# Turning a block ahead of the next scores, dealing the convolution's taps more thinly, and turning tokens by products with diagonals

## The chip, the cores and the metric

The kernel runs on one core of one Trainium2 chip. TensorE (PE) multiplies matrices; VectorE (DVE), ScalarE (ACT) and GpSimd (POOL) work on elements; SyncE (SP) issues the transfers. PE reads its operands from SBUF and writes its products to PSUM banks, which DVE or ACT must empty before they are written again. The metric is the device time of one execution in microseconds, lower being better. Beside the runs stands one profiled execution, from which all durations below come.

## The reference

One step of a streaming encoder: 1024 new frames of a prompt (`x_prompt`) and 32 frames of running streams (`x_sample`), all with 1024 channels. Two branches share one normalised input and one wide projection.

```python
h = rmsnorm(x, norm_g)                            # x / root of the mean square, times g
q = rmsnorm(h @ w_q, q_g) * 64 ** -0.5            # 16 heads of 64
k = rmsnorm(h @ w_k, k_g);  v = h @ w_v
logf = log_sigmoid(h @ w_f + b_f)                 # forget gates; c = cumsum(logf)
u = (h @ w_ua) * sigmoid(h @ w_ub)
ga, gb, ma, mb = (h @ w for w in gate weights)
o = softmax(q k^T + c_q - c_k, causal) v          # by blocks of 128 queries
conv = depthwise causal convolution of u, 31 taps, + b_dw
ya = (o * silu(ga)) @ w_pa
yb = (silu(layernorm(conv, ln_g, ln_b)) * silu(gb)) @ w_pb
y = x + (sigmoid(ma) * ya + sigmoid(mb) * yb) @ w_out
```

The running streams attend to 512 cached keys each besides their own frames. Everything is asked for in f32.

## The kernel before, in words

The projections are computed with f16 halves. A token matrix is split into a high part `xh` and a rest `xl`, a weight tile into `wh` and `wl`, and each product is the sum of three matmuls: xh by wh, xh by wl, xl by wh (all of them stand in `mms`, L183). The tokens are 1024 + 32 = 1056 columns, worked in three chunks of 352; so a "beat" is three matmuls of 352 columns.

**The opening** (`x_split`, up to some 46 us). The tokens arrive as nine tiles `xtok` of 128 tokens by 1024 channels (the ninth has 32 tokens). They must be normalised and turned, so that channels lie on the partitions. For each tile the sum of squares is taken, and its reciprocal root lands in a column of `rs9` (`root`, then `newton`: L509 to L511). `scale` then multiplies half a tile, 128 x 512, by its roots in place (L541): twelve such halves on DVE and six on POOL. `x_split` takes the tiles in three groups of 256, 384 and 416 columns, each in eight slices of 128 channels (`kt`): PE turns the slice of each tile in the group (`nc.tensor.transpose`, L576, against the identity `ident`) into one bank `ptx`; ACT makes xh of it, DVE makes xl (L579); and the first two weight tiles' products with what is ready (L183) follow a few slices behind (`drain`). The `jobs` of a call are lists, by slice, of what is written between; among them are the scalings and the splitting of the weights (L141).

**Projections and attention.** Up to about 570 us PE runs projections. From there to about 1055 us it runs attention: `seq` lists 132 steps, 16 heads by 8 blocks of 128 queries and four steps of the running streams (`Sample`). Step n of the loop at the end of the attention does, in this order: the scores of step n + 3 (`start`, L1121 and L1122, into a bank pair `psS`, of which there are two; DVE then adds the mask, L1124, and takes the negated maximum `nm`, L1126); loads for heads to come; `turn` of step n, which turns the block of probabilities `P` in pieces of 128 x 128 on PE (L1153) into banks `ptr2`, of which there are two (pool `psT`, shared with the values' `po` and the layer norm's `psn`), and copies them to `pt` (L1156), the first four pieces on ACT, the others on DVE; the exponential of step n + 3 (`soft`, ACT, L1133); the normalising of step n + 2 (`norm`: a reciprocal on DVE, L1138, and the product of P with it on POOL, L1139); two beats of a gate's projection as filler; after every second block the values (L1172); two more beats; and one piece of the layer norm, once the convolution is done.

**The convolution's taps** are work for DVE alone: each is one multiply-add over 1086 columns (L371), and they are dealt out by `beat`. Each beat adds `pace["rate"]` to a credit, and each tap takes one off. In attention the rate is `R_A`. The last tap releases the layer norm, whose sums over channels are products `psn` (L1202).

**What sets the order.** PE, DVE and ACT follow the order in which the code is written; in attention SP does too. POOL's order is made by the framework. So an instruction that waits holds up all that is written behind it on its engine.

Of the kernel before, what the change touches and what calls it, by code (L numbers as in the profile page):

```python
# [30 lines left out]
LNO = ((0,), (1, 2), (3,), (4, 5), (6,), (7,), ())  # L31
LNEXP = "natural_log_exp_and_others"
NFILL = 22
R_U, R_V, R_QK, R_G, R_A = 0.21, 0.18, 0.165, 0.23, 0.2
NWARM = 34
HT = TT // 2
HC = HT // 2
# [16 lines left out]
def build(tc, xT, xt, wv, wf, ckT, cv, clT, stT, vec, cst, yT, kT, vO, lfO, cpT, csT):  # L54
# [35 lines left out]
    class Batch:  # L90
# [46 lines left out]
        def high(self, i, wh, raw, ks):  # L137
            nc.scalar.mul(wh[:, ks, :], raw[:, ks, :], self.s[:, i:i + 1])  # L138
# [393 lines left out]
        nc.scalar.activation(y, y, AF.Exp, scale=-0.5)  # L532
        return lambda: newton(rs, v, y)

    def scale(t, h, pool=False):
        r = rows(t)
        x, f = xtok[t][:r, half[h]], rs9[:r, t:t + 1]
        if pool:
            nc.gpsimd.tensor_scalar(x, x, f, 1.0, op0=ALU.mult, op1=ALU.mult)
        else:  # L540
            nc.vector.tensor_scalar(x, x, f, None, op0=ALU.mult)  # L541

    behind = [], []

# [5 lines left out]
    def x_split(c, ws, u, jobs):  # L550


        o, n = XCH[c]
        sl = slice(o, o + n)
        pss = [pj.tile([128, 512], F32, name="pj", tag="pj") for _ in range(2)]

        def project(i, kt):
            mms(pss[i][:, :n], ws[i], X, XL, sl, range(kt, kt + 1), kt == 0, kt == KT - 1)
            if kt < KT - 1:
                return  # L560
            if i == 0:
                for a, b in pieces(o, n):
                    nc.scalar.mul(u[:, b], pss[0][:, a], recs[0].inv)
                return
            nc.vector.tensor_scalar(ua0[:, sl], pss[1][:, :n], recs[1].inv, None, op0=ALU.mult)
            if c == 2:
                for o2, n2, a2 in PCS:
                    b = slice(30 + o2, 30 + o2 + n2)
                    nc.scalar.activation(u[:, b], u[:, b], AF.Sigmoid)
                    nc.vector.tensor_mul(u[:, b], ua0[:, a2:a2 + n2], u[:, b])  # L570

        for kt in range(KT):
            pt = tr.tile([128, 512], F32, name="ptx", tag="tr") if kt % 3 == 2 else st.tile([128, 512], F32, name="ptx", tag="st")
            for j in range((n + 127) // 128):
                r = min(128, n - 128 * j)
                nc.tensor.transpose(pt[:, 128 * j:128 * j + r],  # L576
                                    xtok[o // 128 + j][:r, 128 * kt:128 * kt + 128], ident[:r, :r])
            nc.scalar.mul(xh[:, kt, sl], pt[:, :n], gs[:, kt:kt + 1])
            nc.vector.scalar_tensor_tensor(xl[:, kt, sl], pt[:, :n], gs[:, kt:kt + 1], xh[:, kt, sl],  # L579
                                           op0=ALU.mult, op1=ALU.subtract)  # L580
            for job in jobs.get(kt, ()):
                job()
            for i in range(2):
                behind[i].append(lambda i=i, kt=kt: project(i, kt))
            drain((2, 5 if c == 0 else 2))
# [29 lines left out]
    top(0)  # L615
    total(1)
    step()
    scale(0, 0)
    scale(1, 0, True)
    scale(1, 1, True)  # L620
    scale(0, 1)
    known(0)
    steps_of = {}

# [14 lines left out]
    for f in range(8):  # L639
# [17 lines left out]
        2: [lambda: high(0, 1), lambda: low(0, 1)],  # L657
        3: [lambda: total(2), lambda: known(1), lambda: squares(4)],
        4: [lambda: high(1, 0), lambda: low(1, 0), lambda: rooted(2, 3), lambda: high(0, 2)],
        5: [lambda: steps_of[2](), lambda: scale(2, 0), lambda: scale(3, 0, True), lambda: scale(4, 0), lambda: low(0, 2)],  # L660
        6: [lambda: scale(3, 1, True), lambda: scale(2, 1), lambda: high(1, 1), lambda: low(1, 1)],
        7: [lambda: scale(4, 1), lambda: high(1, 2), lambda: low(1, 2)]})
    x_split(1, ws0, u0, {
        0: [b1.load, b1.load, lambda: squares(5), lambda: squares(6, False)],
        1: [lambda: squares(7)],
        2: [lambda: squares(8)],
        3: [lambda: rooted(5, 4)],
        4: [lambda: steps_of[5](), lambda: scale(5, 0), lambda: scale(6, 0, True)],
        5: [lambda: scale(7, 0), lambda: scale(8, 0), lambda: scale(6, 1, True)],
        6: [lambda: scale(5, 1), lambda: scale(7, 1)],  # L670
        7: [lambda: scale(8, 1), lambda: b1.stage(0)]})
    x_split(2, ws0, u0, {0: [lambda: b1.stage(1)], 2: [consts], 3: [b1.total, b1.power],
                         4: [lambda: b1.split(0)], 5: [lambda: b1.rest(0, 0), lambda: b1.rest(0, 1)],
                         6: [lambda: b1.rest(0, 2), lambda: b1.split(1)]})
# [563 lines left out]
    for n in range(3):  # L1238
# [3 lines left out]
            seq[n - 1].norm()  # L1242
        fill((8, 4, 0)[n])
    for n, b in enumerate(seq):
        if n + 3 < len(seq):
            start(seq[n + 3])
        if n + 9 < len(seq) and getattr(seq[n + 9], "i", 1) == 0:
            seq[n + 9].head.load()
        if n + 6 < len(seq) and isinstance(seq[n + 6], Sample):
            seq[n + 6].load()  # L1250
        if getattr(b, "i", 0) == 3 and b.head.h + 1 < H:
            heads[b.head.h + 1].load_v()
        b.turn()
        if n + 3 < len(seq):
            seq[n + 3].soft()
        if n + 2 < len(seq):
            seq[n + 2].norm()
        some = 2 if isinstance(b, Sample) or b.i > 2 or b.head.h != 8 else 0
        fill(some)
        if n >= 2 and pending(seq[n - 2]):  # L1260
            seq[n - 2].values()
        fill(some)
        if n >= 3 and isinstance(seq[n - 3], Sample):
            seq[n - 3].finish()
        if "ready" in sides:
            next(ln, None)
# [402 lines left out]
```

## Time and profile before

| | |
|---|---|
| median of 3 runs | 1346.9 us (1346.65 to 1347.09) |
| the profiled execution's own time | 1345.89 us |
| its span in the trace | 1344.1 us |
| mean clock of PE in it | 0.996 of full speed |
| PE busy | 1312.6 us, 98% of the span |
| DVE busy | 990.4 us, 74% |
| ACT busy | 719.0 us, 53% |
| POOL busy | 505.8 us, 38% |

The page divides the span among engines and gives, for each group of like instructions, the busy time, the mean time of one in ns, and behind the second bar the idle time of its engine just ahead of them, with what ended it. In the rows of a timeline the first number is the start in us from the span's beginning, the second the duration; what is in square brackets is the wait ahead of it and what ended it. In a row of windows the stretch's bounds come first, then its length, then for each engine the busy time with the count of its instructions.

### The profile page before, as it was taken

Reading aid. Unit: us, or ns where it says so; the run is one execution under the profiler, and the core shown is the slowest. Engines: PE = TensorE matmul, PEld = TensorE weight load, DVE = VectorE, ACT = ScalarE, POOL = GpSimd, SP = SyncE. Lnnn points to the kernel's source line nnn. Section 1 sums busy time; section 2 is a strip of 40 time slices with the busy share of each in tenths; the row PEclk is TensorE's granted clock in tenths of the full one; section 3 lists DMA queues with packets and bytes.
Section 4 is the critical chain, followed back from the end, with each engine's and each line's share of the span. In section 5 each row is a group of like instructions: output and inputs, shape, how many; then the busy total and the mean of one; then the engine's idle time right before and its main releaser. Section 6 shows DMA issues by size and latency. Waiting matters only on the chain.

```text
span 1344.1 us, 24837 instructions
## 1 busy us (share of the span) xinstructions
PE 1312.6 (98%) x9383; PEld 1003.1 (75%) x9383; DVE 990.4 (74%) x1532; ACT 719.0 (53%) x1362; POOL 505.8 (38%) x548
## 2 busy tenths in 40 slices
PE   8999999999999999999889998999999999999999
PEld 5687876666666666667567766777776699999998
DVE  6797879888999997987778866655554489166664
ACT  6644555757676743455555555655555566233320
POOL 2001124547484820243433442222222158255562
PEclk8999999999999999999999999999999999999999
DMA  6343233425352463535644643565452698544462
GB/s 251 98 140 104 93 112 118 139 82 187 95 180 87 162 166 109 160 90 155 165 109 123 186 132 99 147 179 132 131 152 54 240 313 262 176 128 146 142 190 69
DMA packets 113496, 194.97 MB, mean 145 GB/s; under 512 B 34080, under 2 KB 80032, under 8 KB 113376
## 3 DMA queue, kind: packets, MB, share of 16 engines
q1 hardware_dynamic: 113232, 193.31, 46.9%
q8 instruction: 74, 1.21, 0.4%
q14 instruction: 46, 0.38, 0.1%
q10 hardware_dynamic: 144, 0.07, 0.0%
HBM read 127.68 MB, written 65.64 MB: 144 GB/s over the span
## 4 chain that ended last, share of the span: by engine, by line
PE 82%; DVE 9%; ACT 3%; issue 2%; DMA 2%; SPq 1%; POOL 0%; DVEq 0%; ACTq 0%; POOLq 0%
PE pj L183 56%; PE pjv L761 6%; PE pj L1501 6%; PE po L1172 4%; PE ptr L1153 3%; DVE nm L1126 2%; DVE wl L141 2%; DVE y L371 2%; PE psS L1122 2%; PE psS L1121 2%; DMA ga<-s_ga 2%; ACT wh L138 1%; DVE psS L1124 1%; DMA s_q<-qh 1%; PE warm L477 1%
## 5 line engine op out<-in xcount | busy, mean ns | idle before, releaser
L183 PE MATMUL pj<-xh,wh 128*128 128x352 f16 (+2 forms) x1536 | 481.6, 314 | 2.3 <-ACT wh L138 1.4
L183 PE MATMUL pj<-xh,wl 128*128 128x352 f16 (+2 forms) x1536 | 481.2, 313 | 0.7 <-DVE wl L141 0.6
L183 PE MATMUL pj<-xl,wh 128*128 128x352 f16 (+2 forms) x1536 | 480.9, 313 | 0.5 <-DVE xl L579 0.4
L183 PEld LDWEIGHTS <-wh 128*128 128x128 f16 x3072 | 301.5, 98 | 162.1 <-issue 7.1
L371 DVE SCALAR_TENSOR_TENSOR y<-u,vec_t,y 128x1086 f32<-128x1086 f32 x240 | 346.8, 1446 | 12.0 <-ACT y L368 8.9
L1139 POOL TENSOR_SCALAR P<-P,nm 128x128 f32<-128x128 f32 (+7 forms) x128 | 129.9, 1015 | 279.9 <-DVE nm L1138 229.8
L183 PEld LDWEIGHTS <-wl 128*128 128x128 f16 x1536 | 150.5, 98 | 72.0 <-DVE wl L141 1.6
L141 DVE SCALAR_TENSOR_TENSOR wl<-raw,sc,wh 128x384 f16<-128x384 f32 (+1 forms) x192 | 128.2, 693 | 48.3 <-ACT wh L138 48.3
L1133 ACT ACTIVATE P<-psS,nm 128x128 f32<-128x128 f32 (+7 forms) x128 | 95.1, 743 | 113.3 <-DVE nm L1138 70.9
L1126 DVE TENSOR_REDUCE nm<-psS 128x1 f32<-128x128 f32 (+7 forms) x128 | 97.0, 758 | 12.5
L1153 PE MATMUL ptr<-ident,P 128*128 128x128 f32 x576 | 88.6, 276 | 17.3 <-DVE pt L1156 9.2
L175 POOL TENSOR_TENSOR wl<-raw,wh 128x384 fp32r<-128x384 f32 (+1 forms) x51 | 63.3, 1270 | 74.3 <-ACT wh L172 58.6
L1153 PEld LDWEIGHTS ptr<-ident,P 128*128 128x128 f32 x576 | 69.2, 141 | 28.2 <-DVE pt L1156 12.1
L1156 ACT COPY pt<-ptr 128x512 f32<-128x512 f32 (+3 forms) x128 | 64.3, 502 | 44.4 <-PE ptr L1153 43.2
L1121 PE MATMUL psS<-KB,QB 128*128 128x256 f32 (+2 forms) x192 | 81.8, 427 | 0.6 <-ACT P L1133 0.6
L880 POOL TENSOR_TENSOR sql<-sqf,sqh 128x352 fp32r<-128x352 f32 x48 | 57.0, 1187 | 65.8 <-ACT sqh L877 65.8
L138 ACT ACTIVATE wh<-raw,sc 128x1024 f16<-128x1024 f32 (+1 forms) x68 | 73.9, 1091 | 8.2 <-DVE sc L158 7.9
L1172 PE MATMUL po<-pt,V 128*64 128x256 f32 x640 | 72.8, 382 | 2.5 <-ACT pts L1078 1.7
L1124 DVE TENSOR_TENSOR psS<-psS,cmask 128x128 f32<-128x128 f32 x128 | 37.6, 294 | 46.0 <-PE psS L1122 45.6
L906 POOL TENSOR_TENSOR ql<-qn,qh 128x352 fp32r<-128x352 f32 (+1 forms) x48 | 67.8, 1429 | 6.6 <-ACT qh L905 6.5
L761 PE MATMUL pjv<-vwh,xh 128*128 128x260 f16 x256 | 70.1, 274 | 0.0
L761 PE MATMUL pjv<-vwl,xh 128*128 128x260 f16 x256 | 70.0, 273 | 0.0
(271 smaller groups left out, 2532.9 us busy)
## 6 DMA issues: line engine op xcount, KB each, us to landing
raw<-wf SPq DMA_DIRECT2D x92, 512.0 KB
QB<-s_q SPq DMA_DIRECT2D x32, 256.0 KB
KB<-s_k SPq DMA_DIRECT2D x32, 256.0 KB
kT<-qn SPq DMA_DIRECT2D x8, 528.0 KB
s_ga<-t SPq DMA_DIRECT2D x24, 176.0 KB
s_gb<-t SPq DMA_DIRECT2D x24, 176.0 KB
s_ma<-t SPq DMA_DIRECT2D x24, 176.0 KB
s_mb<-t SPq DMA_DIRECT2D x24, 176.0 KB
```

Of the source, the lines that this page charges most:

```text
L138: nc.scalar.mul(wh[:, ks, :], raw[:, ks, :], self.s[:, i:i + 1])
L141: nc.vector.scalar_tensor_tensor(wl[:, ks, :], raw[:, ks, :], self.s[:, i:i + 1], wh[:, ks, :], op0=ALU.mult, op1=ALU.subtract)
L183: nc.tensor.matmul(ps, a[:, kt, :], b(kt, sl), start=(first and n == 0), stop=(last and n == N - 1))
L371: t = nc.vector.scalar_tensor_tensor(y, u[:, i:i + CW], w, y, op0=ALU.mult, op1=ALU.add)
L761: nc.tensor.matmul(ps[:, :VC], a, b, start=(n == 0), stop=(n == 23))
L1121: nc.tensor.matmul(ps[:, b, :wm], QB[:, qsl], KB[:, ksl], start=True, stop=False)
L1126: nc.vector.tensor_reduce(nm[:, 0:1], ps[:, :nb, :w], axis=AX.XY, op=ALU.max, negate=True)
L1133: nc.scalar.activation(P[:, :nk].rearrange("p (b w) -> p b w", b=nb), ps[:, :nb, :w], AF.Exp, bias=nm[:, 0:1], accum_out=nm[:, 1:2])
L1139: nc.gpsimd.tensor_scalar(P[:, :nk], P[:, :nk], nm[:, 2:3], 1.0, op0=ALU.mult, op1=ALU.mult)
L1153: nc.tensor.transpose(pt[:, 128 * j:128 * j + 128], P[:, 128 * (4 * u + j):128 * (4 * u + j) + 128], ident)
L1172: nc.tensor.matmul(po[rows], V[:, j, :], parts[c][:, j, :], start=(c % 2 == 0 and j < 2), stop=(c % 2 == 1 and j >= 2 * c))
L1501: nc.tensor.matmul(pss[c][:, :HC], a[:, k, :], x, start=(not more and kt == 0 and n == 0), stop=(kt == 3 and n == 2), skip_group_check=more)
```

## The change

Three edits stand in the diff.

First, in each attention step `b.turn()` is written at the head of the step, ahead of the scores of step n + 3 and of the loads.

Second, `R_A` is 0.165 in place of 0.2.

Third, in the opening nothing scales the token tiles any more. `diag` makes, for each tile, a 128 x 128 f32 matrix with the tile's roots on its diagonal (DVE, the identity times a column of `rs9`), nine in all, and the turning of a slice is written as a matmul of the tile with its diagonal in place of a transpose against the identity: the product is the turned tile with each token's column times its root. There are 64 such products of 128 x 128 and eight of 32 tokens.

```diff
-R_U, R_V, R_QK, R_G, R_A = 0.21, 0.18, 0.165, 0.23, 0.2
+R_U, R_V, R_QK, R_G, R_A = 0.21, 0.18, 0.165, 0.23, 0.165
...
-    def scale(t, h, pool=False):
-        r = rows(t)
-        x, f = xtok[t][:r, half[h]], rs9[:r, t:t + 1]
-        if pool:
-            nc.gpsimd.tensor_scalar(x, x, f, 1.0, op0=ALU.mult, op1=ALU.mult)
-        else:
-            nc.vector.tensor_scalar(x, x, f, None, op0=ALU.mult)
+    diags = {}
+
+    def diag(*ts):
+        for t in ts:
+            r = rows(t)
+            diags[t] = xip.tile([128, 128], F32, name="diag", tag="diag", bufs=9)
+            nc.vector.tensor_scalar(diags[t][:r, :r], ident[:r, :r], rs9[:r, t:t + 1], None, op0=ALU.mult)
...
-                nc.tensor.transpose(pt[:, 128 * j:128 * j + r],
-                                    xtok[o // 128 + j][:r, 128 * kt:128 * kt + 128], ident[:r, :r])
+                t = o // 128 + j
+                nc.tensor.matmul(pt[:, 128 * j:128 * j + r], xtok[t][:r, 128 * kt:128 * kt + 128], diags[t][:r, :r],
+                                 start=True, stop=True)
...
-    scale(0, 0)
-    scale(1, 0, True)
-    scale(1, 1, True)
-    scale(0, 1)
+    diag(0, 1)
...
-        5: [lambda: steps_of[2](), lambda: scale(2, 0), lambda: scale(3, 0, True), lambda: scale(4, 0), lambda: low(0, 2)],
-        6: [lambda: scale(3, 1, True), lambda: scale(2, 1), lambda: high(1, 1), lambda: low(1, 1)],
-        7: [lambda: scale(4, 1), lambda: high(1, 2), lambda: low(1, 2)]})
+        5: [lambda: steps_of[2](), lambda: diag(2, 3, 4), lambda: low(0, 2)],
+        6: [lambda: high(1, 1), lambda: low(1, 1)],
+        7: [lambda: high(1, 2), lambda: low(1, 2)]})
...
-        4: [lambda: steps_of[5](), lambda: scale(5, 0), lambda: scale(6, 0, True)],
-        5: [lambda: scale(7, 0), lambda: scale(8, 0), lambda: scale(6, 1, True)],
-        6: [lambda: scale(5, 1), lambda: scale(7, 1)],
-        7: [lambda: scale(8, 1), lambda: b1.stage(0)]})
+        4: [lambda: steps_of[5](), lambda: diag(5, 6, 7, 8)],
+        7: [lambda: b1.stage(0)]})
...
     for n, b in enumerate(seq):
+        b.turn()
         if n + 3 < len(seq):
             start(seq[n + 3])
...
             heads[b.head.h + 1].load_v()
-        b.turn()
         if n + 3 < len(seq):
             seq[n + 3].soft()
```

How the instructions stand is shown at three places. The first is PE at the step of block 4 of head 0, between two beats of filler (L183): L1121 and L1122 are the scores of the block three steps ahead (two bank halves, two products each), L1153 the turning of block 4's five pieces (in the changed kernel the lines are L1117, L1118 and L1149). Before:

```order
L183 LDWEIGHTS wh
L183 MATMUL pj<-xl,wh 128x352
L1121 MATMUL psS<-KB,QB 128x512
L1122 MATMUL psS<-KA,QA 128x512
L1121 MATMUL psS<-KB,QB 128x512
L1122 MATMUL psS<-KA,QA 128x512
L1153 MATMUL ptr_7038<-ident,P 128x128 x4
L1153 MATMUL ptr_7044<-ident,P 128x128
L183 LDWEIGHTS wh
```

And changed:

```order
L183 LDWEIGHTS wh
L183 MATMUL pj<-xl,wh 128x352
L1149 MATMUL ptr_7029<-ident,P 128x128 x4
L1149 MATMUL ptr_7035<-ident,P 128x128
L1117 MATMUL psS<-KB,QB 128x512
L1118 MATMUL psS<-KA,QA 128x512
L1117 MATMUL psS<-KB,QB 128x512
L1118 MATMUL psS<-KA,QA 128x512
```

The turning's five pieces moved from behind the four products of the scores to ahead of them.

The second place is DVE in the steps of blocks 5 and 6 of head 0: L1124 adds the mask to the scores three steps ahead, L1126 takes their maximum, L1156 copies the turned pieces beyond the fourth, L1138 is the reciprocal for POOL's normalising, L141 splits a weight tile and L371 is a tap. Before:

```order
L141 SCALAR_TENSOR_TENSOR wl<-raw,sc,wh 128x384
L1124 TENSOR_TENSOR psS<-psS,cmask 128x128
L1126 TENSOR_REDUCE nm<-psS 128x1
L1156 COPY pt<-ptr_7084 128x2x128
L1138 RECIPROCAL nm<-nm 128x1
L141 SCALAR_TENSOR_TENSOR wl<-raw,sc,wh 128x256
L371 SCALAR_TENSOR_TENSOR y<-u,vec_t,y 128x1086
L1124 TENSOR_TENSOR psS<-psS,cmask 128x128
L1126 TENSOR_REDUCE nm<-psS 128x1
L1156 COPY pt<-ptr_7121 128x3x128
```

And changed:

```order
L141 SCALAR_TENSOR_TENSOR wl<-raw,sc,wh 128x384
L1152 COPY pt<-ptr_7077 128x2x128
L1120 TENSOR_TENSOR psS<-psS,cmask 128x128
L1122 TENSOR_REDUCE nm<-psS 128x1
L1134 RECIPROCAL nm<-nm 128x1
L141 SCALAR_TENSOR_TENSOR wl<-raw,sc,wh 128x256
L1152 COPY pt<-ptr_7113 128x3x128
L1120 TENSOR_TENSOR psS<-psS,cmask 128x128
L1122 TENSOR_REDUCE nm<-psS 128x1
```

The copy now stands ahead of the mask and the maximum, and the tap between the two steps has gone to a later place.

The third place is DVE in the opening, from the roots of tiles 2 to 4 (L511) through the next slices; one piece of the difference between the kernels:

```order
 L511 SCALAR_TENSOR_TENSOR rs_185<-rs_185,n_303 128x3
-L541 TENSOR_SCALAR xtok<-xtok,rs_185 128x512 x2
+L541 TENSOR_SCALAR diag<-ident,rs_185 128x128 x3
 L141 SCALAR_TENSOR_TENSOR wl_217<-raw_116,sc,wh_216 128x256
-L579 SCALAR_TENSOR_TENSOR xl<-ptx,gs,xh 128x256
-L541 TENSOR_SCALAR xtok<-xtok,rs_185 128x512
+L580 SCALAR_TENSOR_TENSOR xl<-ptx,gs,xh 128x256
 L141 SCALAR_TENSOR_TENSOR wl_219<-raw_117,sc,wh_218 128x384
-L579 SCALAR_TENSOR_TENSOR xl<-ptx,gs,xh 128x256
-L541 TENSOR_SCALAR xtok<-xtok,rs_185 128x512
+L580 SCALAR_TENSOR_TENSOR xl<-ptx,gs,xh 128x256
```

Four scalings of 512 columns became three diagonals of 128, and the xl of the next slices stand that much sooner; on PE the products keep the places of the transposes. Elsewhere the last tap stands in head 8 in place of head 6, and the layer norm's products `psn` in head 10 among beats of filler in place of head 8, where the code leaves the filler out in three steps (`b.head.h != 8`).

## The prediction

> **What bounds the kernel now.** First the profile page: the share of each engine, the chain that ended last, and the costliest group.
>
> ```profile
> span 1344.1 us, 24837 instructions
> PE 1312.6 (98%) x9383; PEld 1003.1 (75%) x9383; DVE 990.4 (74%) x1532; ACT 719.0 (53%) x1362; POOL 505.8 (38%) x548
> PE 82%; DVE 9%; ACT 3%; issue 2%; DMA 2%; SPq 1%; POOL 0%; DVEq 0%; ACTq 0%; POOLq 0%
> L183 PE MATMUL pj<-xh,wh 128*128 128x352 f16 (+2 forms) x1536 | 481.6, 314 | 2.3 <-ACT wh L138 1.4
> ```
>
> PE is busy in 1312.6 of 1344.1 us and carries 82% of the chain. So two things alone move the time: work that PE gets or loses, and its 31.5 us of idleness. Busy time by stretches tells where these lie (opening, then attention; the columns after the stretch are its length, then PE, PEld, DVE, ACT, POOL, the granted clock and the DMA).
>
> ```profile
> 10.00:20.00 10.00, 7.51 (x38) 4.89 (x37) 7.16 (x19) 8.55 (x21) 1.27 (x4) 0.66 1.04 390
> 20.00:30.00 10.00, 8.67 (x66) 6.41 (x65) 7.81 (x16) 6.73 (x16) 1.14 (x2) 1.00 0.36 147
> 30.00:40.00 10.00, 9.46 (x61) 5.94 (x59) 7.85 (x21) 6.92 (x13) 2.40 (x3) 1.00 0.00 1
> 40.00:50.00 10.00, 10.00 (x62) 6.03 (x61) 6.95 (x14) 6.20 (x10) 0.27 (x1) 1.00 0.19 57
> 570.00:700.00 130.00, 119.18 (x875) 85.67 (x875) 100.99 (x193) 71.15 (x155) 51.25 (x58) 1.00 0.47 127
> 700.00:800.00 100.00, 97.29 (x744) 70.44 (x741) 75.76 (x145) 56.70 (x121) 41.17 (x50) 1.00 0.55 153
> 800.00:900.00 100.00, 94.53 (x659) 68.61 (x658) 64.10 (x161) 59.45 (x135) 25.64 (x45) 0.98 0.51 136
> 900.00:1000.00 100.00, 99.42 (x754) 72.69 (x752) 53.11 (x131) 55.82 (x122) 24.63 (x48) 1.00 0.51 136
> 1000.00:1055.00 55.00, 53.43 (x426) 37.69 (x425) 27.97 (x65) 29.71 (x61) 12.44 (x19) 1.00 0.25 76
> ```
>
> In the opening PE fills up: idle 1.33 us in the second of these stretches, 0.54 in the third, nothing in the fourth. In attention it idles for 10.82 + 2.71 + 5.47 + 0.58 + 1.57 = 21.2 us. The waits of PE say on what: the whole run's group of turning products, then the waits from 570 to 800 us (two rows) and from 800 to 1055 (two rows).
>
> ```profile
> L1153 PE MATMUL ptr<-ident,P 128*128 128x128 f32 x576 | 88.6, 276 | 17.3 <-DVE pt L1156 9.2
> PE ptr L1153 <- DVE pt L1156: 7.8, 8, 1.7
> PE ptr L1153 <- ACT pt L1156: 3.2, 3, 1.1
> PE ptr L1153 <- ACT pt L1156: 3.2, 2, 2.2
> PE ptr L1153 <- DVE ot L1177: 1.2, 1, 1.2
> ```
>
> Of the 21.2 us, 17.3 stand ahead of turning: PE wants a bank that an earlier step's copy has not emptied. That is what the change touches in attention.
>
> **The opening: what a product costs.** Each of 72 transpositions becomes a product with a diagonal. No f32 product of this shape is in the trace, so its price is bounded by rows: three transpositions and the matmul behind them, the f32 products of the running tokens, and the weight loads of another f32 product.
>
> ```profile
> 26.48 0.49 PE L576 MATMUL ptx<-ident,xtok 128*128 128x128 f32 x3
> 26.81 0.33 PE L183 MATMUL pj<-xh,wh 128*128 128x384 f16 x1
> 70.81 1.08 PE L716 MATMUL pjs<-vraw,xsm 128*32 128x260 f32 x16
> L716 PE MATMUL pjs<-vraw,xsm 128*32 128x260 f32 x64 | 4.3, 389 | 0.0
> L1202 PEld LDWEIGHTS psn<-mean,ones_f 128*128 128x128 f32 x6 | 1.0, 189 | 0.4 <-ACT mean L1211 0.3
> ```
>
> A transposition takes (26.81 - 26.48)/3 = 0.11 us and has one record (576 of them in the row of attention, which has 16 x 36). The code issues 32 products at L716 and the trace has 64 records: an f32 product runs as two. Sixteen records, four abreast, take 1.08 us, so one of 260 columns at most 0.27, and of 128 columns about 0.13 with the start in it. The low end is one record's 0.11 for the whole product (nothing added); the high end is two weight loads of 0.19 that hide nothing, 0.38 (0.27 added). I take two records at the transposition's own pace, 0.22: 0.11 added per tile, since the pace of the L716 records lies near it.
>
> Where it counts: the second token group has 8 x 3 tiles, and the third 8 x 3 and eight small ones; both lie where PE is almost never idle. 24 x 0.11 = 2.6, and 2.6 + 0.4 (half the price for the small ones) = 3.0 us. The first group's 16 tiles (1.8 us) stand in a stretch where PE idles 2.5 us of ten behind ACT and DVE: 0.5 on the path.
>
> Against it stand scalings that go: 12 on DVE and 6 on POOL, replaced by nine diagonals. The rows, in order of time: the copy of the identity, of a diagonal's size; then a pair of scalings, the waits behind such work, and, from the chain, where the matmuls after the third group start.
>
> ```profile
> 4.90 0.22 DVE L504 COPY ident<-cst_t 128x128 f32<-128x128 f32 x1
> 19.26 1.33 DVE L541 TENSOR_SCALAR xtok<-xtok,rs 128x512 f32<-128x512 f32 x2
> 21.33 0.47 DVE L579 SCALAR_TENSOR_TENSOR xl<-ptx,gs,xh 128x256 f16<-128x256 f32 x1
> 21.86 0.33 PE L576 MATMUL ptx<-ident,xtok 128*128 128x128 f32 x1 [1.30 <-DVE xl L579]
> 33.86 0.33 PE L576 MATMUL ptx<-ident,xtok 128*128 128x128 f32 x1 [0.50 <-DVE xl L579]
> 46.08 17.59 PE pj L183 x114
> ```
>
> At 19.26 two scalings of 1.33 us become three diagonals of 0.22, 0.66: DVE comes 0.67 us sooner to the xl that PE waits for. I take 0.7 off the 1.30. The wait of 0.50 goes whole, as its DVE work shrinks likewise; 0.3 more for the first two diagonals at 8 us and small idleness. The opening: 2.6 + 3.0 + 0.5 - 1.5 = **+4.6 us**. Ends: if a product costs what a transposition does, all 1.87 us of idleness may go, -1.9; at 0.27 added, 48 x 0.27 + 1 + 0.5 - 1.5 = +13. Nothing hides the tiles afterwards: from 40 to 50 us, right behind the third group, PE is busy in 10.00 of 10.00.
>
> [...]
>
> **Attention: turning first.** In a step PE now turns before it takes the scores. Two waits move with it. The copy of the turned tile on DVE moves ahead of the mask's addition and the reduction, so banks come free sooner; but PE comes to them sooner by the scores. One case, the wait of 1.74 us:
>
> ```profile
> 589.02 0.40 PE L1121 MATMUL psS<-KB,QB 128*128 128x256 f32 x1
> 590.97 0.29 DVE L1124 TENSOR_TENSOR psS<-psS,cmask 128x128 f32<-128x128 f32 x1
> 591.57 0.41 DVE L1156 COPY pt<-ptr 128x256 f32<-128x256 f32 x1
> 592.04 0.33 PE L1153 MATMUL ptr<-ident,P 128*128 128x128 f32 x1 [1.74 <-DVE pt L1156]
> ```
>
> The copy could start at 590.97, 0.6 us sooner; PE stands at its bank from 589.02 on and not from 589.67, 0.65 sooner. Nothing gained: I put the banks at 0.
>
> The other is POOL's normalizing, which must have ended before the turn. At seven steps it ended after the scores had started, where the turn will now stand. The first, the worst and the last of the seven:
>
> ```profile
> 571.26 1.39 POOL L1139 TENSOR_SCALAR P<-P,nm 128x128 f32<-128x128 f32 x1 [12.69 <-DVE nm L1138]
> 572.23 0.39 PE L1121 MATMUL psS<-KB,QB 128*128 128x512 f32 x1
> 645.55 2.28 POOL L1139 TENSOR_SCALAR P<-P,nm 128x768 f32<-128x768 f32 x1 [4.81 <-DVE nm L1138]
> 646.54 0.39 PE L1121 MATMUL psS<-KB,QB 128*128 128x256 f32 x1 [0.44 <-ACT P L1133]
> 1005.48 1.41 POOL L1139 TENSOR_SCALAR P<-P,nm 128x768 f32<-128x768 f32 x1 [3.40 <-DVE nm L1138]
> 1006.46 0.39 PE L1121 MATMUL psS<-KB,QB 128*128 128x256 f32 x1 [0.19 <-ACT P L1133]
> ```
>
> PE would wait 0.42, 1.29 and 0.43 us there, and 3.4 over the seven: +3.4 (the waits of 0.44 and 0.19 on ACT's P, ahead of the scores, only pass to the turn). Behind the waiting turn stand the scores, and behind these DVE's reduction and ACT's exponential, so lateness is passed on; the group of turning products holds 17.3 of the 21.2 us of idleness, so PE hardly waits for the scores' banks now, and I add nothing. SP keeps its order but for a store of the convolution, and POOL its norms; the next head's loads are issued nine steps ahead, behind one turn more at most: 0.
>
> **Thinner taps.** The rate falls from 0.2 to 0.165, by 17.5%; the taps last to the ninth head, not the seventh.
>
> ```profile
> sum 485.00, DVE 59.95; mean DVE 5.45
> ```
>
> That is the taps' DVE time in attention. It stays 60 us, spread wider. The 7.8 us of waits on DVE's copies up to 800 us fall with the rate: -1.4 (ends: 0, and -7.8 if they all vanish). The layer norm moves with the last tap: its products stand in head 10 among fillers instead of in head 8, which has none in three steps. Of the 4.4 us of waits on turning that stand after 800 on ACT and ot, most in that place, I take off 1.0. Attention: 3.4 - 1.4 - 1.0 = **+1.0 us** (ends: -12, if 12 of the 17.3 go, and +9, if every one of the seven waits is the worst and nothing is gained).
>
> **Sum.** The profiled execution took 1345.89 us (span 1344.1 and 1.8 around it), 1.0 under the median of 1346.9. 1345.9 + 4.6 + 1.0 = 1351.5; against the median **1352.5 us**.
>
> **Rivals.**
> 1. The taps were what made DVE late, and a copy at the head of DVE's step comes in time: 12 of the 17.3 us go, half of POOL's 3.4 stays. For it: eight of these waits up to 800 us, 7.8 us together, name a pt copy of DVE. Against it: DVE is busy only 101 of 130 us even at the worst, so single collisions and not load make the waits. -10.3 + 4.6 = -5.7: 1341 us. It decides from an attention gain of 7.3 us on, so that over 0.2% is left (2.7 us, about what a measurement here tells from no change).
> 2. POOL becomes the wait: the reduction, and with it the reciprocal that POOL waits for, now stands behind a copy (0.41 us in the row above) on DVE. If each of the seven steps then waits as the worst does, 7 x 1.29 = 9.0 in place of 3.4, attention is +6.6: 1345.9 + 4.6 + 6.6 + 1.0 = 1358 us. For it: POOL waits 12.69, 4.81 and 3.40 us for nm in the three rows above, so it starts as late as DVE lets it. Against it: the group of turning products names DVE and ACT ahead of its idleness, not POOL.
> [...]
> 4. The products cost nothing: a record each, or hidden: -1.5, attention +1.0, 1346.5 us. The low clock of 0.66 from 10 to 20 us, if products fill PE enough to lift it, helps here.
>
> **How the numbers follow.** The forecast 0.48 (1348 to 1357 by itself), the rivals 0.17, 0.12, 0.10, 0.13. Within 0.2% (1344.2 to 1349.6) lie rival 4 and 0.06 of the forecast: 0.19. Faster: 0.17; slower: 0.64. The range 1343 to 1361 leaves out most of rival 1 and most of rival 3, some 0.2.
>
> **What would show it.** Twice 72 records of the turning products in the opening, and the first matmul after the third group (46.0 us now) at about 50.6: right in the opening; at 46 or earlier rival 4, past 56 rival 3. PE's waits ahead of turning: about 3 us newly on POOL's P, and on the pt copies near 16: right. On POOL over 8 us: rival 2. Under 7 in all: rival 1. Wrong altogether if PE's idleness in attention falls under 12 us.

## The result, and the profile after

The changed kernel takes 1362.4 us (median of four runs, 1362.22 to 1363.69), beside 1347.0 us for the kernel before on the same chip: a ratio of 1.0096 (95% interval 1.0078 to 1.0114). It is slower, by 1.0%; the medians lie 15.4 us apart, and their own quotient, 1.0114, is the upper end of that interval. The forecast was 1352.5 with a range to 1361: the sign came true, the size did not, and the time lies above the range. The profiled execution took 1363.69 us, the slowest of the four, with a span of 1361.9 us, 17.8 us longer than the span of the kernel before.

The page of the changed kernel, in the three lines that answer to those shown of before:

```profile
PE 1325.1 (97%) x9455; PEld 1002.3 (74%) x9455; DVE 985.3 (72%) x1529; ACT 715.5 (53%) x1362; POOL 504.6 (37%) x542
PE 84%; DVE 7%; ACT 4%; issue 2%; DMA 1%; POOL 0%; SPq 0%; DVEq 0%; ACTq 0%; POOLq 0%
L1149 PE MATMUL ptr<-ident,P 128*128 128x128 f32 x576 | 88.8, 278 | 23.4 <-ACT pt L1152 9.9
```

PE is busy for 12.5 us more (1312.6 before), in 72 more records, those of the turning products. The idleness ahead of turning in attention did not fall: 17.3 before, 23.4 now, and ACT's copy is named first where it was DVE's.

Where the time went is told by two views. The first is the chain, at the matmuls behind the third group, which stood at 46.08 us before:

```profile
50.43 17.59 PE pj L183 x114
```

So the opening costs 4.35 us. The second is the table by stretches, for the whole attention, from the first scores to the last value; the kernel before, then the changed one:

```profile
565.88:1052.64 486.76, 465.62 (x3458) 336.45 (x3457) 324.29 (x697) 274.54 (x594) 154.54 (x217) 1.00 0.48 130
```

```profile
570.24:1070.36 500.12, 473.54 (x3458) 328.28 (x3457) 323.30 (x697) 270.79 (x594) 160.62 (x217) 0.98 0.47 127
```

Attention is 13.4 us longer, with the same 3458 matmul records; with the opening's 4.35 us that is 17.7 of the 17.8 us between the spans. Its idleness grew by 5.4 us (500.12 - 473.54 = 26.6 from 486.76 - 465.62 = 21.1), and PE's busy time by 7.9 us for the same work. The mean granted clock fell from 1.00 to 0.98. The stretches show where:

```profile
570.00:700.00 130.00, 121.87 (x874) 83.28 (x873) 94.61 (x186) 69.83 (x151) 46.57 (x54) 0.99 0.44 121
800.00:900.00 100.00, 89.88 (x608) 62.35 (x602) 60.08 (x133) 53.68 (x117) 32.30 (x44) 0.97 0.53 140
900.00:1000.00 100.00, 97.05 (x719) 67.80 (x719) 58.88 (x150) 56.93 (x131) 25.18 (x45) 0.98 0.41 115
```

The granted clock in the trace is either whole or half (1.00 or 0.50 throughout both kernels). Before, one spell of half clock lies in attention, 3.41 us long; now there are five of 3.41 us each. Within the spell at 898.10 us the matmuls of a beat start 0.29 us apart, and 0.15 behind it; so a spell does half of 3.41 us of work, and by this estimate four more cost 6.8 us. With 5.4 us of idleness that is 12.2 of the 13.4 us; 1.2 us are not assigned. The waits of PE in the changed kernel, the largest five (`pt` is the copy of turned probabilities, `P` POOL's normalising, `os_t` and `pts` belong to the steps of the running streams):

```profile
PE ptr L1149 <- ACT pt L1152: 9.9, 7, 3.1
PE ptr L1149 <- POOL P L1135: 7.0, 4, 2.7
PE ptr L1149 <- DVE os_t L1098: 3.0, 2, 2.3
PE po L1168 <- ACT pts L1074: 2.3, 2, 1.5
PE ptr L1149 <- DVE pt L1152: 1.8, 2, 1.1
```

The many waits of 1 us on DVE's copies (9.2 us in eleven) are nearly gone. A few long ones have taken their place: six pass 2.3 us, and four of these are followed by a spell of half clock (the fifth spell follows two waits of 0.57 and 1.14 us that stand close together).

### The profile page after: what moved, and what is told of

Read it like the earlier page. It is cut to its first block, busy times and chain, and to the rows that moved or that the text cites. A ratio compares the mean times of both kernels' runs of the same rounds, so it can differ in the third digit from the quotient of the medians.

```text
span 1361.9 us, 24934 instructions
## 1 busy us (share of the span) xinstructions
PE 1325.1 (97%) x9455; PEld 1002.3 (74%) x9455; DVE 985.3 (72%) x1529; ACT 715.5 (53%) x1362; POOL 504.6 (37%) x542
## 4 chain that ended last, share of the span: by engine, by line
PE 84%; DVE 7%; ACT 4%; issue 2%; DMA 1%; POOL 0%; SPq 0%; DVEq 0%; ACTq 0%; POOLq 0%
PE pj L183 57%; PE pjv L757 6%; PE pj L1497 6%; PE po L1168 5%; PE ptr L1149 3%; PE psS L1117 2%; PE psS L1118 2%; DVE nm L1122 2%; DVE wl L141 1%; ACT wh L138 1%; DVE y L371 1%; PE ptx L577 1%; ACT P L1129 1%; DMA s_y<-y 1%; DVE psS L1120 1%
## 5 line engine op out<-in xcount | busy, mean ns | idle before, releaser
L183 PE MATMUL pj<-xh,wh 128*128 128x352 f16 (+2 forms) x1536 | 484.1, 315 | 2.0 <-ACT wh L138 1.2
L183 PE MATMUL pj<-xh,wl 128*128 128x352 f16 (+2 forms) x1536 | 482.3, 314 | 0.7 <-DVE wl L141 0.7
L183 PE MATMUL pj<-xl,wh 128*128 128x352 f16 (+2 forms) x1536 | 482.2, 314 | 0.6 <-DVE xl L580 0.3
L183 PEld LDWEIGHTS <-wh 128*128 128x128 f16 x3072 | 301.6, 98 | 182.2 <-issue 23.9
L371 DVE SCALAR_TENSOR_TENSOR y<-u,vec_t,y 128x1086 f32<-128x1086 f32 x240 | 345.6, 1441 | 11.9 <-ACT y L368 8.8
L1135 POOL TENSOR_SCALAR P<-P,nm 128x128 f32<-128x128 f32 (+7 forms) x128 | 135.2, 1056 | 288.0 <-DVE nm L1134 265.4
L183 PEld LDWEIGHTS <-wl 128*128 128x128 f16 x1536 | 151.2, 98 | 70.2 <-DVE wl L141 1.1
L141 DVE SCALAR_TENSOR_TENSOR wl<-raw,sc,wh 128x384 f16<-128x384 f32 (+1 forms) x192 | 126.9, 687 | 50.9 <-ACT wh L138 50.9
L1149 PE MATMUL ptr<-ident,P 128*128 128x128 f32 x576 | 88.8, 278 | 23.4 <-ACT pt L1152 9.9
L1122 DVE TENSOR_REDUCE nm<-psS 128x1 f32<-128x128 f32 (+7 forms) x128 | 97.0, 758 | 12.5
L1149 PEld LDWEIGHTS ptr<-ident,P 128*128 128x128 f32 x576 | 70.9, 143 | 39.4 <-ACT pt L1152 10.1
L1117 PE MATMUL psS<-KB,QB 128*128 128x256 f32 (+2 forms) x192 | 77.5, 405 | 0.0
L120 POOL CAST topb<-tops 128x2 bf16<-128x2 f32 x35 | 18.5, 528 | 158.3 <-ACT junk L117 108.4
L757 PE MATMUL pjv<-vwh,xl 128*128 128x260 f16 x256 | 69.9, 273 | 0.0
```

The costliest lines, as they stand in the source:

```text
L141: nc.vector.scalar_tensor_tensor(wl[:, ks, :], raw[:, ks, :], self.s[:, i:i + 1], wh[:, ks, :], op0=ALU.mult, op1=ALU.subtract)
L183: nc.tensor.matmul(ps, a[:, kt, :], b(kt, sl), start=(first and n == 0), stop=(last and n == N - 1))
L371: t = nc.vector.scalar_tensor_tensor(y, u[:, i:i + CW], w, y, op0=ALU.mult, op1=ALU.add)
L757: nc.tensor.matmul(ps[:, :VC], a, b, start=(n == 0), stop=(n == 23))
L1117: nc.tensor.matmul(ps[:, b, :wm], QB[:, qsl], KB[:, ksl], start=True, stop=False)
L1122: nc.vector.tensor_reduce(nm[:, 0:1], ps[:, :nb, :w], axis=AX.XY, op=ALU.max, negate=True)
```

## The experiments

The kernels were run beside the kernel before on the same chip, whose own median was 1349.8 to 1351.8 us on the chips of these runs; so ratios are compared, not times. "Idle" is PE's idleness in attention and "spells" the number of stretches of half clock in it, both from each run's trace; a spell lasts one window of 3.41 us or two.

| run | edits | ratio to before (95%) | idle, us | spells |
|---|---|---|---|---|
| e1 | turn first | 1.0100 (1.0084 to 1.0117) | 29.2 | 6 |
| e2 | rate 0.165 | 0.9961 (0.9946 to 0.9976) | 22.9 | 1 |
| e3 | diagonals | 1.0020 (1.0008 to 1.0032) | 22.3 | 1 |
| e4 | turn first, rate 0.165 | 1.0073 (1.0060 to 1.0087) | 26.4 | 5 |
| e8 | all three, again | 1.0112 (1.0094 to 1.0129) | 26.2 | 4 |
| e5 | e4 and late exponential | 0.9869 (0.9855 to 0.9883) | 8.3 | 0 |
| e6 | e2 and late exponential | 0.9881 (0.9866 to 0.9895) | 9.5 | 0 |
| e7 | diagonals made, transposes kept | 0.9990 (0.9978 to 1.0002) | 21.9 | 3 |
| e9 | late exponential alone | 0.9895 (0.9877 to 0.9914) | 12.5 | 1 |
| e10 | all three and late exponential | 0.9890 (0.9875 to 0.9906) | 8.5 | 0 |
| e11 | e1 and late exponential | 0.9886 (0.9868 to 0.9905) | 11.8 | 0 |
| e12 | e5, filler left out in head 10 | 0.9851 (0.9835 to 0.9867) | 8.2 | 0 |

### Each edit alone

e1 to e4 take single hunks of the diff: e1 the moved `b.turn()`, e2 the line of `R_A`, e3 the opening, e4 the first two.

> Only the turn is moved ahead of the scores; the taps' rate and the opening are those of before. Theory A (the loss of attention lies in the turn's new place, which puts PE behind POOL's normalizing and behind the copies of the running streams' steps): slower, by the 7.0 us of POOL waits and 3.0 us of os_t waits that the changed trace shows, less the 7 us of DVE waits that went: +2 to +6 us, and 1.7 us more for every spell of half clock. Theory B (the loss comes from the layer norm's landing in head 10 because the taps are thinner): within 2 us of before, or faster, with the layer norm in heads 8 and 9 again.

> Only the taps' rate falls to 0.165. Theory A: DVE's late copies fall a little, about -1 us to +1 us. Theory B: the layer norm lands among the fillers of head 10 here too, so most of the changed kernel's loss in attention (8.3 us in head 10) comes with it: +6 to +10 us.

> Only the opening's products with diagonals. If the opening's price is its own, the first matmul after the third group stands at 50.4 us as in the changed kernel (46.1 before), and the whole is +4.4 us, since the work behind it is bound by PE and only shifts. A rival: the shift also moves the idle stretches of attention against the grid on which the clock is halved; then spells come or go and the whole differs from +4.4 by a multiple of 1.7 us.

> Both edits of attention, the opening as before. If the parts add up, the changed kernel's +15.5 less the opening's 4.4: +11 us. The spells of half clock fall where more than about 1.7 us of idleness lies within one window of 3.41 us; the windows stand differently to the work here, so their number may differ from the changed kernel's five, each worth 1.7 us.

Turning first alone makes the kernel 1.0% slower; that is as much as the whole change. The thinner taps make it faster by 0.4%. The three edits alone add up to +0.8%; within the intervals that agrees with the whole. So theory B falls, and theory A holds as to the edit, though not as to what is waited for: POOL's normalizing costs 0.5 us in e1, and ACT's copies more than anything else (6.4 us before).

```profile
PE ptr L1153 <- ACT pt L1156: 15.3, 11, 4.4
PE ptr L1153 <- DVE pt L1156: 4.4, 5, 1.9
```

Theory B's landing of the layer norm in head 10 is real, and e2's trace has two waits in heads 10 and 11 too (2.29 us at 889.19 and 1.74 us at 922.86, of the kind of 3.11 and 2.33 us in the changed kernel); turning first makes each of them longer by some 0.6 to 0.8 us.

Why turning first makes waits longer can be read from one step that e2 and e4 reach at the same time, that of block 4 of head 3, which is turned in five pieces. PE and ACT in e2 (turn behind the scores):

```profile
679.26 0.47 PE L1121 MATMUL psS<-KB,QB 128*128 128x512 f32 x1
680.27 0.60 PE L1153 MATMUL ptr<-ident,P 128*128 128x128 f32 x4
681.93 0.33 PE L1153 MATMUL ptr<-ident,P 128*128 128x128 f32 x1 [1.06 <-ACT pt L1156]
678.72 1.01 ACT L1133 ACTIVATE P<-psS,nm 128x896 f32<-128x896 f32 x1 [0.50 <-DVE nm L1138]
681.29 0.58 ACT L1156 COPY pt<-ptr 128x512 f32<-128x512 f32 x1
```

The same in e4 (turn first):

```profile
678.92 0.60 PE L1153 MATMUL ptr<-ident,P 128*128 128x128 f32 x4
681.95 0.33 PE L1153 MATMUL ptr<-ident,P 128*128 128x128 f32 x1 [2.43 <-ACT pt L1156]
682.03 0.48 PE L1121 MATMUL psS<-KB,QB 128*128 128x512 f32 x1
678.74 1.01 ACT L1133 ACTIVATE P<-psS,nm 128x896 f32<-128x896 f32 x1 [1.79 <-DVE nm L1138]
681.31 0.58 ACT L1156 COPY pt<-ptr 128x512 f32<-128x512 f32 x1
```

ACT copies the first four pieces at 681.3 in both, and the fifth waits for their bank: the other one still holds the turned result of a running stream (L1099), half of which DVE copies only at 683.3. ACT's queue holds, ahead of this copy, the exponential of the scores two steps on (678.7), a weight's high half and an evacuation; the exponential waits for `nm`, and that for scores which PE computed in the step before. None of this came sooner. PE turned 1.35 us sooner and so waited 1.37 us longer for the same copy, and the scores, which it used to compute in that time, start at 682.03 in place of 679.26, and all that hangs on them starts later too.

e3's trace gives the opening as in the changed kernel (the matmuls behind the third group at 50.54 us). Over its runs it costs 0.20%, which is 1.1 to 4.3 us of 1352: less than the 4.4 that two traces show; the last section has the likely reason.

### The copy ahead of the exponential

e5 and e6 take the waiting exponential out of the copy's way: in step n, behind the copy, the exponential of step n + 2 is written, where that of step n + 3 stood. One exponential still stands between two copies, but its scores are a step older when ACT comes to it. The edit in e5 (in e6 the turn stays behind the scores):

```diff
     for n, b in enumerate(seq):
         b.turn()
+        if n + 2 < len(seq):
+            seq[n + 2].soft()
         if n + 3 < len(seq):
             start(seq[n + 3])
...
-        if n + 3 < len(seq):
-            seq[n + 3].soft()
         if n + 2 < len(seq):
             seq[n + 2].norm()
```

> As e4 (turn first, rate 0.165, opening of before), but the exponential of step n + 2 is issued in step n behind the copy of the turned tile, not in step n - 1 ahead of it. Theory C (turning first loses because ACT's copy is queued behind the exponential of the scores just ahead, so PE only arrives earlier at the same moment): the waits on ACT's pt copies fall from 11.1 us in e4 to under 4, the spells of half clock with them, and the time falls by 8 us or more below e4. Theory A' (POOL's normalizing and the steps of the running streams are the cause): the ACT waits return under another name, and the time stays within 3 us of e4.

> As e2 (rate 0.165, the turn behind the scores as before), with the exponential one step later behind the copy. Theory C: the ACT waits of e2 (4.4 us) go too, but they are smaller, so the time falls by 1 to 5 us below e2; against e5 it shows what the turn's place is worth once the copy is free.

Both are faster than the kernel before, by 1.3% and 1.2%; e5 fell below e4 by more than the 8 us that theory C asked for (1.0073 to 0.9869, some 27 us). Attention in e5, and the waits of PE in it:

```profile
565.87:1037.35 471.48, 463.16 (x3458) 324.64 (x3457) 329.58 (x697) 269.29 (x592) 164.44 (x217) 1.00 0.50 135
```

```profile
PE ptr L1153 <- POOL P L1139: 3.6, 5, 2.1
PE ptr L1153 <- ACT pt L1156: 3.0, 4, 1.0
PE ptr L1153 <- DVE pt L1156: 0.2, 1, 0.2
```

The waits on ACT's copies fell from 11.1 to 3.0 us and no spell is left in attention. That the exponential was what held up the copies is seen in ACT's own waits for `nm` ahead of it, from 560 to 1080 us in e4 and then in e5:

```profile
ACT P L1133 <- DVE nm L1138: 167.6, 107, 4.0
ACT P L1133 <- DVE nm L1138: 5.4, 5, 3.5
```

PE's idleness in attention fell by 18.1 us from e4 to e5, of which 8.1 us had named ACT's copies; the waits on the streams' steps (`os_t`, `pts`) and on DVE's copies went with them. In the step shown above the copy now comes ahead of that exponential:

```profile
672.54 0.60 PE L1153 MATMUL ptr<-ident,P 128*128 128x128 f32 x4
673.81 0.33 PE L1153 MATMUL ptr<-ident,P 128*128 128x128 f32 x1 [0.68 <-ACT pt L1156]
673.17 0.59 ACT L1156 COPY pt<-ptr 128x512 f32<-128x512 f32 x1
673.65 1.01 ACT L1133 ACTIVATE P<-psS,nm 128x896 f32<-128x896 f32 x1
```

The second step of theory C, that e6 would gain only 1 to 5 us on e2, was a miss: it gained 0.8%, some 11 us. So the kernel before suffers from the same queue, and turning first made it worse.

### What is left of each edit once the copy is free

> The kernel before with the late exponential alone (rate 0.2, turn behind the scores). If the exponential ahead of the copy is the whole cause of the waits, most of the gain of e6 comes without the thinner taps: -10 to -17 us against before, no spell of half clock in attention. If the thinner taps are needed for it, it stays within 6 us of before.

> The changed kernel whole, with the late exponential. Attention as in e5 (471 us from its first scores to its last value), the opening as in the changed kernel (third group at 50.4 us): if opening and attention add up, 3 to 5 us above e5's 1331.6, so about 1335.5, and some 29 us below the changed kernel.

> Turn first and late exponential, taps at the old rate of 0.2. With the copy free, what is left of DVE's lateness shows: if the taps matter only where the copy hangs, within 2 us of e5; if POOL's normalizing behind a late reciprocal is the next bound, it waits more than e5's 3.6 us and the time is 2 to 6 us above e5.

> As e5, but the three steps without filler stand in head 10, where the layer norm's products now are, and not in head 8. If the layer norm's bank and its DVE work make PE wait among fillers, 1 to 2 us below e5; if the filler covers these waits, 1 to 3 us above it.

e9 alone brings 1.05%, most of the gain, though one spell and 7.5 us of waits on DVE's copies are left. e11 against e9 (1336.6 and 1337.1 us, their ranges overlap) shows no difference for turning first at the old rate; e5 against e6 (1331.6 and 1333.0, ranges apart: up to 1331.81 and from 1332.30) gives it 1.4 us at the new one. So the edit that lost 1% is worth nothing to 0.1% in the other order. e11's POOL waits are 5.6 us beside 3.6 in e5, as the second theory there had it, and e11 has 3.5 us more idleness in all. Its ratio lies 0.0017 above e5's, some 2 us, with intervals that overlap, so the times don't decide between the two theories.

e10 holds all of the changed kernel: its attention takes 471.7 us beside e5's 471.5, and its third group ends at 50.62 us, much as in the changed kernel (50.43). Its span is 4.9 us longer than e5's, and the third group ends 4.55 us later: in the traces opening and attention add up. Its ratio is 0.0021 above e5's, some 3 us, the low end of what was expected, and 2.2% below that of e8.

e12 did not differ from e5 by more than the intervals; it is the fastest ratio of all, 0.9851.

### The opening taken apart

> The diagonals are made and the scalings are gone as in e3, but the tiles are turned by transposes against the identity as before: the multiplication of the tokens by their roots is left out. If the opening's price is that of the products (0.11 us more for each of 56 tiles) less what the missing scalings free, the third group ends 1.2 to 1.9 us before that of before (46.1 us there), since the waits of 1.30 and 0.50 on DVE's xl go; if the scalings were no load, it ends at 46.1.

```diff
-                nc.tensor.matmul(pt[:, 128 * j:128 * j + r], xtok[t][:r, 128 * kt:128 * kt + 128], diags[t][:r, :r],
-                                 start=True, stop=True)
+                nc.tensor.transpose(pt[:, 128 * j:128 * j + r], xtok[t][:r, 128 * kt:128 * kt + 128], ident[:r, :r])
```

In e7's chain the matmuls behind the third group stand 2.05 us earlier than before (46.08), a little more than expected:

```profile
44.03 17.59 PE pj L183 x114
```

So the missing scalings free 2.05 us, and the products cost 50.43 - 44.03 = 6.4 us. That is a net price: e7, like the kernel before, spends 6.83 us of its opening at half clock, and the changed kernel none. One product in the changed kernel, where six records are three products:

```profile
26.05 0.83 PE L577 MATMUL ptx<-diag,xtok 128*128 128x128 f32 x6
26.72 0.33 PE L183 MATMUL pj<-xh,wh 128*128 128x384 f16 x1
```

(26.72 - 26.05)/3 = 0.223 us: twice a transposition's 0.11.

That the scalings weigh more than their own duration is seen on DVE. In the kernel before, while POOL scaled (19.38 to 21.14 us):

```profile
20.51 0.90 DVE L141 SCALAR_TENSOR_TENSOR wl<-raw,sc,wh 128x256 f16<-128x256 f32 x1
```

And in e7, where POOL has nothing to do then:

```profile
19.57 0.48 DVE L141 SCALAR_TENSOR_TENSOR wl<-raw,sc,wh 128x256 f16<-128x256 f32 x1
```

### The changed kernel a second time

> The changed kernel itself, for a ratio on this chip and a second profile. If the halving of the clock follows a grid of 3.41 us that runs free of the program, the idle waits stand at the same places as in the first profile (2.43, 2.65, 2.41, 3.11, 2.33, 2.43 us) but the spells begin elsewhere and their number may differ from five; if the clock follows the waits themselves, the same five places show it.

Five of the six waits above 2.3 us stand at the same places (2.43, 2.61, 3.09, 2.64 and 2.43 us; that of 2.41, at block 4 of head 8, fell to 0.94). The spells are not the same. Those at 597.72 and 833.24 are missing, one at 821.34 is new, and two last for two windows. The new one follows the wait of 2.61 us in head 8, which was 2.65 us in the first profile and had no spell behind it: there it lay 1.61 us in one window of 3.41 us and 1.05 in the next, here 1.70 us lie in one. So the length of a wait doesn't settle it; how the wait falls into the windows counts too.

## Why the prediction was wrong

**The opening** came out close to what was worked: +4.6 forecast, +4.35 in the trace. The price of a product (0.11 added, taken from the pace of the L716 records) was right: 0.223 beside 0.11. The terms were each a little small: products 6.1 forecast and 6.4 measured, scalings 1.5 and 2.05, perhaps since the slowing of DVE by POOL was in no row that I used. Part of the agreement is luck: the sum had no term for the clock, and the 6.4 us hold what the products gave back by ending the half clock of 6.83 us. Only rival 4 had named the low clock there. What rival 3 stands for, a third group that ends past 56 us, no run shows: it ended at 50.43, and a product took 0.223 us.

**"Nothing gained: I put the banks at 0"** is the step that failed. It was worked out on one wait for a copy of DVE, whose place in the order moves with the turn. ACT's copy of the first four pieces was left out. It stands in the order behind the exponential of a later step, which hangs on scores, and moving the turn does not move it. In the pair of e2 and e4 the wait grew by all that PE came sooner, 1.37 us, and the scores were held up besides. As a total the waits on copies even fell: in the changed kernel those on DVE's went from 9.2 to 1.8 us while those on ACT's rose from 6.4 to 9.9. But the ones on ACT became long, at block 4 of heads 3 and 15 from 1.05 and 1.04 us to 2.43 each, and half clock followed four of the six waits above 2.3 us. The steps of the running streams, in no term of the sum, brought 3.0 us more on `os_t`. The bound of +9 for attention did not reach this, since it let the seven waits on POOL grow and no others.

**The half clock** is the term that the sum does not have, and the largest part of the miss: attention was forecast at +1.0 us and came out at +13.4, and four more spells cost 6.8 us of it, more than the added idleness of 5.4. The rows of before had it: the stretch of 800 to 900 us at a clock of 0.98.

**POOL's normalizing** was forecast at 3.4 us at seven steps; 7.0 us came, at four steps, one of them among the seven (block 5 of head 2, 0.48 us). So the term was half of what came, and it had the places wrong. At the two longest waits POOL ends late because of what DVE does just then. At the largest, that of 2.65 us in head 8:

```profile
818.84 1.74 POOL L1135 TENSOR_SCALAR P<-P,nm 128x256 f32<-128x256 f32 x1 [4.07 <-DVE nm L1134]
818.97 1.34 DVE L371 SCALAR_TENSOR_TENSOR y<-u,vec_t,y 128x1086 f32<-128x1086 f32 x1
875.62 0.48 POOL L1135 TENSOR_SCALAR P<-P,nm 128x256 f32<-128x256 f32 x1 [2.81 <-DVE nm L1134]
```

POOL waits 4.07 us for the reciprocal, which on DVE stands behind a copy and a reduction, as rival 2 had it, and then the product of 256 columns takes 1.74 us under a tap, where it takes 0.48 without one. The other long wait on POOL, 2.41 us, goes back to a transfer: DVE stood 3.19 us for the head's gate (at 828.46) with the reciprocal queued behind. That gate is still waited for in e5 and e12; loading it earlier was not tried.

**Thinner taps** were forecast at -1.4 and the layer norm's move at -1.0. e2 is faster by 0.24 to 0.54% over its runs, some 3 to 7 us. But its trace shows an attention of 486.9 us beside 486.8 before, and the two waits at the layer norm. The kernel before has one trace, and in it two windows with 1.74 and 1.93 us of idleness were not followed by half clock; its runs on other chips spread from 1345.8 to 1354.5 us, while e5's lie within 1.2 us. The mean granted clocks of the runs tell more: 0.9931 over the 17 runs of before on e2's chip, 0.9957 over e2's six. By an estimate (the part of the clock not granted, times the span) that is 9.4 and 5.8 us lost to half clock, and the mean spans, 1349.9 and 1345.3 us, differ by 4.6. So most of e2's gain is less half clock; which waits became shorter is not shown, as there is no trace of a slower run of before.

**Rival 1** (the waits on DVE's copies go) had the right fact and the wrong price: the waits on DVE's copies did go (9.2 to 1.8 us), and others took their place. It took both edits of attention, which leave 2.7 us in e4; turning first alone leaves 4.4 in e1, and the rate alone 9.5 in e2.

## What to carry to other kernels

When an instruction is moved ahead on one engine, look at what stands ahead of its consumer on the other engines' queues: if that hangs on something that did not move, the wait grows by all that was gained, and what stood between is late besides. Here the remedy was to issue each exponential a step later, when its scores are ready, and it was worth 1.05% alone and 1.3% with the other edits of attention, in a kernel whose PE was already busy for 98% of its span. And a few waits of 2 us cost more here than many of 1 us, since half clock for a window of 3.41 us followed most of them (four of the six above 2.3 us in the changed kernel).

## What the runs showed of the hardware

**The clock follows a grid.** All spells of a run begin at whole multiples of 3.413 us from each other: in the changed kernel those of attention stand 69, 88, 99 and 134 such windows behind the first, at 597.72. In its second execution (e8) the grid lies about half a window off that of the first, with a spell at 896.43 in place of 898.10, though attention begins only 0.32 us later (570.56 beside 570.24). One example in the changed kernel: the window with the wait of 3.11 us, and the next.

```profile
894.68:898.10 3.42, 0.33 (x3) 0.09 (x1) 1.41 (x4) 2.40 (x5) 0.91 (x1) 1.00 1.15 243
898.10:901.51 3.41, 3.40 (x10) 2.05 (x11) 2.00 (x6) 0.00 (x0) 0.00 (x0) 0.50 0.67 229
```

And the kernel before, two windows with much the same idleness, 1.82 and 1.93 us, of which the first is followed by half clock and the second not:

```profile
822.10:825.51 3.41, 1.59 (x8) 1.03 (x8) 3.31 (x7) 0.48 (x1) 0.00 (x0) 1.00 0.19 73
825.51:828.93 3.42, 3.42 (x14) 2.39 (x13) 1.88 (x4) 1.85 (x4) 0.80 (x1) 0.50 0.66 157
832.34:835.75 3.41, 1.48 (x10) 1.04 (x11) 2.49 (x6) 1.88 (x4) 0.00 (x0) 1.00 0.14 53
835.75:839.17 3.42, 3.42 (x28) 2.71 (x26) 3.21 (x11) 2.50 (x7) 1.89 (x2) 1.00 0.02 5
```

Over the attention of the fourteen traces, 32 windows at full clock have 1.70 us or more of idleness, and 27 are followed by half clock; all thirteen of 2.0 us or more are; no window at full clock with less than 1.70 us is. What decides between 1.7 and 2.0 stays open. So does why six spells last two windows: in four of them the first window has only 0.34 to 0.63 us of idleness. In the kernel before there are three such windows of 1.70 us or more (1.74, 1.82 and 1.93 us, of which the second is followed by half clock), in the changed kernel five (1.71, 1.79, 1.84, 2.41 and 3.09 us, all followed).

**Transpositions and the clock.** In the opening all ten traces with transpositions have a spell between 11 and 28 us, and none of the four with products has one: from 5 to 30 us the mean clock is 0.80 to 0.93 in the ten and 1.00 in the four. The stretch from 5 to 30 us before, and in the changed kernel:

```profile
5.00:30.00 25.00, 21.15 (x132) 14.65 (x131) 18.43 (x49) 18.53 (x44) 5.09 (x9) 0.86 0.77 296
```

```profile
5.00:30.00 25.00, 21.06 (x160) 16.56 (x161) 16.35 (x48) 18.62 (x44) 1.70 (x5) 1.00 0.77 295
```

PE's busy share is the same, the clock is not. Since work at half clock takes longer (before, a transposition starts 0.21 us after the last at 17.4 us, and 0.11 after it at 26.5), single windows of the grid are the better comparison: the one just ahead of the spell before, and one of the changed kernel:

```profile
9.73:13.14 3.41, 1.99 (x15) 1.31 (x14) 2.75 (x6) 3.41 (x8) 0.66 (x2) 1.00 1.03 412
```

```profile
14.04:17.45 3.41, 1.99 (x15) 1.26 (x15) 2.31 (x7) 2.62 (x8) 0.27 (x1) 1.00 1.06 337
```

PE is busy for 1.99 us in both; half clock follows the first and not the second. That the scalings are not the cause is shown by e7, which has none and keeps the transpositions: its spell begins at 13.04 us. The last slice of the third group starts between 45.8 and 47.9 us in the nine full kernels with transpositions and between 50.2 and 50.5 in the four with products; so an opening with products costs between 2.2 and 4.7 us by these traces, which is likely why e3's ratio gave less than 4.4. The granted clocks agree: by the same estimate as above e3's twelve runs lost 6.0 us to half clock, and the runs of before on that chip 9.4. Equal busy time did not bring an equal clock here, and the amount of transposing alone does not explain it: in e4 a window of the opening with 1.46 us of idleness and 0.05 us of transpositions was followed by half clock, and one with 0.96 and 0.93 was not. How transpositions act on the clock stays open.

**DVE and POOL slow each other**: the splitting of 128x256 weights on DVE took 0.90 us while POOL scaled and 0.48 us in e7, where it did not; POOL's product of 256 columns took 1.74 us under a tap of DVE and 0.48 without one. No run here shows by what they do so.
